# Two heads' softmax rows transposed side by side, and one reading engine per half of a PSUM bank

## The chip, the cores and the metric

The kernel runs on one core of one Trainium2 chip. The metric is the device time of one execution in microseconds (us), from the start of the program on the core to its end. The engines are named as the profile names them: PE (TensorE, the matrix engine; its weight loads are listed apart as PEld), DVE (VectorE), ACT (ScalarE), POOL (GpSimd) and SP (SyncE, which issues transfers).

## What is computed

One decoder layer on 1024 tokens of width 1024, in float32: a normalisation with a shift and scale from a conditioning vector, one input projection, an attention group of 8 query heads that share 2 key/value heads (4 heads to each), a short gated convolution group, an output projection, and a feed-forward block. The attention has three branches, and the part that matters here is the product of each branch's probabilities with its values:

```
p_c = masked_softmax(q . kc * scale + bias_c)      # 63 compressed keys
p_s = masked_softmax(q . ks * scale + bias_s)      # the causal keys (with 16 blocks, all are selected)
p_w = masked_softmax(q . kw * scale + bias_w)      # the last 512 keys
o   = g0 * (p_c @ vc) + g1 * (p_s @ vs) + g2 * (p_w @ vw)
```

The gates g come from a sigmoid of the projection.

## The kernel before

Every product is made of float32r halves: a tensor is split into a rounded part (`hi`) and its remainder (`lo`), and the products of the parts are added in PSUM. V is kept with both parts side by side, 64 columns of `hi` and 64 of `lo`, so a product with V gives 128 rows, which are folded to 64 at the end.

All instructions are recorded by a planner (class `Plan`): each operation has a cost, the engines that may do it and the operations that it must follow. The planner makes a list schedule, and the instructions are then issued in that order on every engine. So a changed cost or a changed dependence moves instructions on all engines. A dependence is found in `op` (line 116) from the memory that the operations touch; for PSUM the whole bank counts as one place (line 77), and only a write makes a dependence (line 131). The cost of a matmul is set in `mm` (line 307), that of a transpose on PE in `pet` (line 314).

The attention works on units of one pair of heads `hp` (both heads of a pair share the same K and V) and 256 queries `m`. `attention` (line 1112) makes four rows for it: 128 queries each, two query blocks `qp` and two heads `hl`. `row` (line 924) makes the scores of one row on PE, adds the bias and finds the maximum on DVE, takes exp on ACT, scales by gate over sum on POOL or ACT, and returns the blocks: one of 64 keys (the compressed branch, on 64 partitions once transposed) and up to 13 of 128 keys, each with its block of V. The rows lie in a buffer that holds four of the longest. `pv` (line 983) then takes groups of up to four blocks: it transposes them on PE into one of two PSUM banks (`tp_r`: the banks `sc2` and `stb`), copies the bank as `hi` on ACT, subtracts for `lo` on DVE, and multiplies: for every block a product of V with 128 columns of `hi` and one with 128 of `lo`, all added into the bank `po`. At the end of a unit `po` is folded into the output with two copies on ACT and two additions on DVE. There are 16 such units (`supers`, line 1110).

While the rows go through DVE and ACT, PE is given other products in between: conv products with the first eight units, and the first half's output projection and 30 tiles of the first feed-forward product with the other eight (`products`, line 999). They accumulate into the banks `fa0`, `fa1` and `sc3`. The planner decides where each stands.

Ahead of the attention, `raws` (line 706) copies the raw K and V of the compressed branch from four PSUM banks: four copies from each bank, each copy on ACT or DVE as the planner chooses.

Of the kernel before, what the change touches and what calls it, by code (L numbers as in the profile page):

```python
# [14 lines left out]
PSUM = bass.MemoryType.PSUM  # L15
# [18 lines left out]
def f32(ap):  # L34
    return ap.bitcast(F)
# [11 lines left out]
class Plan:  # L47
# [68 lines left out]
    def op(self, alts, outs, ins, nbytes=0, port=(), weight=1):  # L116
        o = Op(alts, len(self.ops), nbytes)
        o.weight = weight
        o.port = port
        o.group = self.group  # L120
        for aps, wr in ((ins, False), (outs, True)):
            for ap in aps:
                if not hasattr(ap, "tensor"):
                    continue
                key = ap.tensor.name
                if ap.space == DRAM and key not in self.scratch:
                    continue
                m = self._mask(ap)
                log = self.mem.setdefault(key, [])
                for po, pm, pw in log:  # L130
                    if (wr or pw) and po is not o and self._hit(m, pm):
                        if po.end is None:
                            o.preds.add(po)
                        else:
                            o.past.append((po, *po.end))
                if wr:
                    log[:] = [e for e in log if e[0] is o or not self._covers(m, e[1])]
                log.append((o, m, wr))
        self.ops.append(o)
        return o  # L140
# [165 lines left out]

    def mm(self, out, a, b, start, stop):
        n, m = self._n(out), self._n(a)
        c = max(0.4375 * n + 3, 58.0)
        if a.dtype == F and n > 128:  # L310
            c *= 4
        self.op([("PE", c, lambda: self.nc.tensor.matmul(out, a, b, start=start, stop=stop))], [out], [a, b])  # L312
# [30 lines left out]
    def tt(self, out, a, b, op, engs=("DVE",)):  # L343
        n, alts = self._n(out), []
        for e in engs:
            if e == "DVE":
                alts.append((e, 1.04 * n + 68, lambda: self.nc.vector.tensor_tensor(out, a, b, op)))  # L347
            else:
                alts.append((e, 2.11 * n + 148, lambda: self.nc.gpsimd.tensor_tensor(out, a, b, op)))
        self.op(alts, [out], [a, b], port=("POOL",) if self._ps(a, b) else ("DVE", "POOL"))  # L350
# [91 lines left out]
def hymba_layer(ctx: ExitStack, tc: tile.TileContext, xT, cT, w_first, w_cols, w_vg, w_ada, w_ada2, b_ada,  # L442
# [3 lines left out]
    P = Plan(tc)  # L446
    P.ahead = AHEAD
    mult, add, subt, amax, amin = ALU.mult, ALU.add, ALU.subtract, ALU.max, ALU.min
# [59 lines left out]
    ident, qpair = FA2[:, FA2N - 640:FA2N - 512], RA[:, RAN - 128:]  # L508
# [3 lines left out]
    h = [[Region(RA, H0 + 8192 * hf + 4096 * i, H0 + 8192 * hf + 4096 * i + 4096)(8, 512) for i in range(2)] for hf in range(2)]  # L512
# [105 lines left out]
    acc = [[sc_t[0], sc_t[1]], [sc_t[2], sc_t[3]], fa_t]  # L618
# [23 lines left out]
    craws = [Cr(2, T) for _ in range(2)]  # L642
# [63 lines left out]
    def raws(i):  # L706

        for hf in range(2):
            for g in range(2):
                r, c = slice(64 * g, 64 * g + 64), 512 * hf  # L710
                P.copy(craws[i][0:64, g, c:c + 512], acc[i][hf][r], ("ACT", "DVE"))
                f = 1 - hf
                P.copy(craws[i][64:128, g, c - 1 + f:c + 511], acc[i][hf][r, f:512], ("ACT", "DVE"))

    def compress(i):
        craw, cpe = craws[i], cpe_r()
# [136 lines left out]
    while c0 < TROW:  # L853
        n = min(512, TROW - c0)
# [39 lines left out]
    def prow(w):  # L894
        if pb[0] + w > PB:
            pb[0] = 0
        pb[0] += w
        return pbuf[:, pb[0] - w:pb[0]]
# [25 lines left out]
    def row(hp, m, qp, hl, q):  # L924
        qt = 2 * m + qp
        tt, te, tg = tabs[2 * hp + hl]
        kall, kw0, _, vt, sc_r = half1 if m >= 2 else half0
        nf, w0 = 128 * (qt + 1), max(0, qt - 4)
        nw = 128 * (qt - w0 + 1)
        s = prow(64 + nf + nw)  # L930
        mx, nm, den, cf = mx_r(), nm_r(), den_r(), cf_r()

        tab0, te0 = 896 - 128 * qt, 64 + nf
        cmp = (64, tg[:, 56 - 8 * qt:120 - 8 * qt], 0, 0)

        def full(a, b):
            return b - a, tt(tab0 + a, tab0 + b), 64 + a, 1

        if qt in (3, 7):
            jobs = [([(KC0 + a, 512)], [full(a, a + 512)]) for a in range(0, nf, 512)]  # L940
            last = [(0, 64)], [cmp]
        else:
            n0 = min(nf, 448)
            jobs = [([(0, 64 + n0)], [cmp, full(0, n0)])]
            last = ([(512, nf - n0)], [full(n0, nf)]) if nf > n0 else ([], [])
        if qt >= 4:
            jobs.append(([(kw0 + 128 * w0 + 128, 512)], [(512, tt(512, 1024), te0 + 128, 2)]))
            te_ = [(kw0 + 128 * w0, 128)], [(128, te, te0, 2)]
            if sum(n for _, n in last[0]) <= 384:
                last = last[0] + te_[0], last[1] + te_[1]  # L950
            else:
                jobs.append(te_)
        else:
            jobs.append(([(kw0, nw)], [(nw, tt(tab0, tab0 + nw), te0, 2)]))
        seen = set()
        for mms, sums in jobs + [last]:
            if not mms:
                continue
            a, c = sc_r(), 0
            for k0, n in mms:  # L960
                for i in range(2):
                    P.mm(a[:, c:c + n], q[:, hl, i, qp * 128:qp * 128 + 128], kall[:, k0:k0 + n], i == 0, i == 1)
                c += n
            c = 0
            for n, tab, ro, br in sums:
                P.ttr(s[:, ro:ro + n], a[:, c:c + n], tab, mx[:, br:br + 1] if br in seen else 2 * NEG, mx[:, br:br + 1])
                seen.add(br)
                c += n
        P.ts(nm, mx, -1.0, -0.1 * NEG, mult, amin, engs=EW)
        rs = [slice(0, 64), slice(64, 64 + nf), slice(64 + nf, 64 + nf + nw)]  # L970
        for br in (1, 2, 0):
            P.act(s[:, rs[br]], s[:, rs[br]], AF.Exp, bias=nm[:, br:br + 1], accum=den[:, br:br + 1])
        P.ts(den, den, 1e-30, 0.0, amax, add, engs=EW)
        P.recip(cf, den)
        P.tt(cf, cf, gates[:, qt, (2 * hp + hl) * 3:(2 * hp + hl) * 3 + 3], mult, EW)
        for br in (1, 2, 0):
            P.ts(s[:, rs[br]], s[:, rs[br]], cf[:, br:br + 1], 0.0, mult, add, engs=("POOL", "ACT"))
        vF, vW = ([vt[:, k, b] for k in range(qt + 1)] for b in range(2))
        return [(s[:, rs[1]][:, 128 * k:128 * k + 128], vF[k]) for k in range(qt + 1)] + \
            [(s[:, rs[0]], vc[hp // 2][0:64])] + \  # L980
            [(s[:, rs[2]][:, 128 * (k - w0):128 * (k - w0) + 128], vW[k]) for k in range(w0, qt + 1)]

    def pv(oo, blocks):

        parts = [b for b in blocks if b[0].shape[-1] == 128]
        parts = [[b for b in blocks if b[0].shape[-1] < 128]] + [parts[i:i + 4] for i in range(0, len(parts), 4)]
        for gi, part in enumerate(parts):
            n, w = 128 * len(part), part[0][0].shape[-1]
            tp, hi, lo = tp_r()[0:w, 0:n], hl_r()[0:w, 0:n], hl_r()[0:w, 0:n]
            for i, (p, _) in enumerate(part):  # L990
                P.pet(tp[:, 128 * i:128 * i + 128], p, ident)
            P.copy(hi, tp)
            P.sub(lo, tp, f32(hi))
            for i, (_, v) in enumerate(part):
                c = slice(128 * i, 128 * i + 128)
                P.mm(oo, v, hi[:, c], gi + i == 0, False)
                P.mm(oo, v, lo[:, c], False, gi == len(parts) - 1 and i == len(part) - 1)

# [113 lines left out]
    def attention(hp, m, q):  # L1112

        acc = po_r()
        o = at0[hp][:, 256 * m:256 * m + 256] if m < 2 else ot_r()
        for i in range(4):
            pv(acc[:, 128 * i:128 * i + 128], row(hp, m, i % 2, i // 2, q))
        for hl in range(2):
            r, c = slice(64 * hl, 64 * hl + 64), slice(256 * hl, 256 * hl + 256)
            P.copy(o[r], acc[r, c])  # L1120
            P.tt(o[r], acc[64 - 64 * hl:128 - 64 * hl, c], o[r], add)
        if m >= 2:
            c = 256 * (m - 2)
            hi, lo = (h[1][i][:, 4 + hp, c:c + 256] for i in range(2))
            P.copy(hi, o, ("ACT", "DVE"))
            P.sub(lo, o, f32(hi), EW)
# [5 lines left out]
    for u, (hp, ms) in enumerate(supers):  # L1132
# [9 lines left out]
        for m in ms:  # L1142
            q = q_r()
# [45 lines left out]
    with ExitStack() as pf:  # L1189
# [32 lines left out]
        for ch in range(4):  # L1222
            for j in range(8):
                w = load_w(w_ff1[ch * 8 + j])
# [10 lines left out]
            for c in range(8):  # L1235
                w = load_w(w_ff2[ch, c])
# [90 lines left out]
```

## Time and profile before

| | us |
|---|---|
| median of 3 runs (1434.29 to 1435.71) | 1435.21 |
| the profiled execution's own time | 1435.77 |
| its span, first to last instruction | 1434.0 |
| PE busy (share of the span) | 1397.4 (97%) |
| DVE busy | 781.6 (55%) |
| ACT busy | 644.8 (45%) |
| mean granted TensorE clock | 0.987 |

The span falls into stages: to about 75 us the normalisation and the first products; to 215 us the compression, the window keys, values and queries; from 215 to 830 us the attention with the other products in between; to 885 us the rest of the second half's output projection; and then the feed-forward block to the end. A matmul's row in the trace gives its start and how long it is in the array; since several are in the array at a time, the price of one is read from the distance between starts, and not from that duration.

### The profile page before, as it was taken

The page shows a single profiled execution, that of the slowest core. Times are in us where ns is not written, and L with a number is a line of the kernel's source. Part 1 is how long each engine was busy: PE and PEld are TensorE (multiplying, and loading weights), DVE is VectorE, ACT ScalarE, POOL GpSimd, SP SyncE. Part 2 cuts the span into 40 slices and gives each one's busy share as a digit, 9 for nine tenths or more (in the row PEclk, how much of TensorE's full clock was granted, in tenths as well). Part 3 has the DMA queues.
Part 4 walks back from the last instruction along what each step waited for, and adds up shares of the span by engine and source line. Part 5 has one row for each costly group of instructions (what it writes and reads, how often), then busy time and mean ns, then how long its engine had stood idle before and what let it go on. Part 6 is the DMA issues. An engine that isn't in the chain of part 4 may idle for free.

```text
span 1434.0 us, 19643 instructions
## 1 busy us (share of the span) xinstructions
PE 1397.4 (97%) x7016; PEld 1141.2 (80%) x7016; DVE 781.6 (55%) x1928; ACT 644.8 (45%) x1362; POOL 114.3 (8%) x221
## 2 busy tenths in 40 slices
PE   5999999999999999999999997999999999999998
PEld 2778777887887888888888886888888888888887
DVE  5987876667576686555555457451531352243122
ACT  5776656665465676655755545330130122103110
POOL 0001001111121111101111100000000000000000
PEclk8999999999999999999999998999999999999999
DMA  9478884353252213433322541450430232123031
GB/s 346 129 216 239 288 265 155 103 163 106 69 185 75 90 40 96 148 121 98 110 84 82 176 133 67 146 169 30 127 109 30 75 119 72 59 69 106 32 118 59
DMA packets 91606, 175.72 MB, mean 123 GB/s; under 512 B 10745, under 2 KB 30754, under 8 KB 90996
## 3 DMA queue, kind: packets, MB, share of 16 engines
q1 hardware_dynamic: 87764, 159.65, 34.3%
q0 software_dynamic: 3744, 14.81, 3.3%
q8 instruction: 55, 0.90, 0.3%
q14 instruction: 43, 0.35, 0.1%
HBM read 145.48 MB, written 32.61 MB: 124 GB/s over the span
## 4 chain that ended last, share of the span: by engine, by line
PE 90%; DMA 4%; DVE 2%; ACT 1%; issue 1%; SPq 1%; DVEq 0%; ACTq 0%
PE pd L312 37%; PE fa L312 23%; PE sc L312 16%; PE po L312 9%; PE stb L315 3%; PE sc L315 2%; DMA d_tab<-d_row 1%; ACT FA L330 1%; DVE FA L358 1%; DVE RA L347 1%; DMA FA<-in_w_cols 1%; SPq L397 1%; DMA FA<-in_w_ada 1%; DVE FA L347 0%; DMA FA<-in_xT 0%
## 5 line engine op out<-in xcount | busy, mean ns | idle before, releaser
L312 PE MATMUL fa<-RA 128*128 128x512 f32 (+1 forms) x1384 | 463.3, 419 | 1.1 <-DVE RA L347 1.1
L312 PE MATMUL pd<-RA 128*128 128x512 f32 x1392 | 413.8, 393 | 7.4 <-ACT RA L336 4.3
L336 ACT CAST RA<-FA 128x512 fp32r<-128x512 f32 (+5 forms) x235 | 163.0, 708 | 491.8 <-PE pd L312 286.3
L312 PE MATMUL sc<-RA 128*128 128x512 f32 (+6 forms) x1328 | 357.3, 371 | 12.0 <-DVE RA L338 9.8
L347 DVE TENSOR_TENSOR RA<-FA,RA 128x512 fp32r<-128x512 f32 (+5 forms) x327 | 246.7, 773 | 166.6 <-PE pd L312 95.5
L312 PEld LDWEIGHTS pd<-RA 128*128 128x128 f32 x1392 | 262.4, 190 | 66.3 <-ACT RA L336 5.0
L312 PE MATMUL pd<-hid,RA 128*128 128x512 f32 x960 | 310.4, 389 | 0.0
L312 PEld LDWEIGHTS fa<-RA 128*128 128x128 f32 (+1 forms) x1384 | 250.6, 190 | 42.6 <-DVE RA L347 1.6
L312 PEld LDWEIGHTS sc<-RA 128*128 128x128 f32 x1328 | 236.1, 191 | 54.2 <-DVE RA L338 10.6
L312 PEld LDWEIGHTS pd<-hid,RA 128*128 128x128 f32 x960 | 180.2, 188 | 37.4
L312 PE MATMUL po<-RA 128*128 128x128 f32 (+1 forms) x1092 | 206.4, 266 | 0.1
L312 PEld LDWEIGHTS po<-RA 128*128 128x128 f32 (+1 forms) x1092 | 185.4, 193 | 18.0 <-DVE RA L347 0.5
L358 DVE SCALAR_TENSOR_TENSOR FA<-pd,mod,FA 128x512 f32<-128x512 f32 x64 | 46.4, 748 | 199.5 <-PE pd L312 199.5
L330 ACT ACTIVATE FA<-FA,nm 128x64 f32<-128x64 f32 (+6 forms) x192 | 114.6, 599 | 31.5 <-DVE nm L366 31.5
L377 DVE CUSTOM_DVE_ANT_0 FA<-sc,FA 128x512 f32<-128x512 f32 (+5 forms) x192 | 82.8, 455 | 43.3 <-PE sc L312 41.9
L330 ACT ACTIVATE FA<-FA 128x512 f32<-128x512 f32 (+2 forms) x147 | 89.1, 618 | 21.3 <-DVE FA L358 11.7
L347 DVE TENSOR_TENSOR RA<-stb,RA 128x512 fp32r<-128x512 f32 (+4 forms) x108 | 60.7, 562 | 47.3 <-PE po L312 29.4
L315 PE MATMUL stb<-FA,FA 128*128 128x128 f32 (+1 forms) x332 | 84.3, 283 | 0.0
L370 POOL TENSOR_SCALAR FA<-FA,cf 128x64 f32<-128x64 f32 (+8 forms) x97 | 59.5, 620 | 200.1 <-DVE cf L347 150.3
L336 ACT CAST RA<-sc 64x128 fp32r<-64x128 f32 (+3 forms) x108 | 44.4, 411 | 68.2 <-PE sc L315 54.8
L336 ACT CAST RA<-stb 128x512 fp32r<-128x512 f32 (+4 forms) x108 | 52.1, 483 | 48.0 <-PE po L312 30.3
L347 DVE TENSOR_TENSOR RA<-sc,RA 64x128 fp32r<-64x128 f32 (+3 forms) x108 | 50.8, 470 | 33.5 <-ACT RA L336 28.0
(123 smaller groups left out, 961.5 us busy)
## 6 DMA issues: line engine op xcount, KB each, us to landing
FA<-in_w_ff SPq DMA_DIRECT2D x64, 512.0 KB, 4.3
FA<-in_w_ada SPq DMA_DIRECT2D x64, 256.0 KB, 3.1
FA<-in_w_ff SPq DMA_DIRECT2D x60, 256.0 KB, 2.7
FA<-in_w_cols SPq DMA_DIRECT2D x34, 256.0 KB, 3.4
FA<-in_xT SPq DMA_DIRECT2D x32, 256.0 KB, 5.0
FA<-in_w_ada SPq DMA_DIRECT2D x16, 512.0 KB, 5.6
d_q<-FA SPq DMA_DIRECT2D x32, 256.0 KB, 4.7
RA<-d_q POOLq DMA_DIRECT2D x16, 512.0 KB, 4.7
```

Source lines behind the costliest of these rows:

```text
L312: self.op([("PE", c, lambda: self.nc.tensor.matmul(out, a, b, start=start, stop=stop))], [out], [a, b])
L315: self.op([("PE", 110.0, lambda: self.nc.tensor.transpose(out, a, ident))], [out], [a, ident])
L330: self.op([("ACT", c, lambda: self.nc.scalar.activation(out, a, func, **kw))], outs, ins)
L336: alts.append((e, 0.833 * n + (53 if ps else 93), lambda: self.nc.scalar.copy(out, a)))
L347: alts.append((e, 1.04 * n + 68, lambda: self.nc.vector.tensor_tensor(out, a, b, op)))
L358: self.op([("DVE", 1.04 * self._n(out) + 68 + 61 * ptr, lambda: self.nc.vector.scalar_tensor_tensor(out, a, s, b, op0, op1, **kw))], [out] ...
L370: alts.append((e, 0.833 * n + 174 + 83 * ptr, lambda: self.nc.gpsimd.tensor_scalar(out, a, s1, s2, op0, op1)))
L377: self.op([("DVE", 1.04 * self._n(out) + 75, lambda: self.nc.vector.tensor_tensor_reduce(out, a, b, 1.0, init, ALU.add, ALU.max, accum))], ...
L397: self.op([(q, c, lambda: e.dma_start(out=out, in_=a))], [out], [a], nbytes=n, weight=2 if within else 1)
```

## The change

`pv` now takes the rows of both heads of one query block. A group is two blocks of each head (four transposes into one bank), with the two heads' transposed blocks side by side, and each product streams 256 columns, 128 of either head, against the block of V that both share. `attention` calls it twice for a unit instead of four times, and the fold reads strided halves of `po`. In `raws` the copies from one half of a bank's partitions are all on ACT, those from the other all on DVE. The planner counts two readers of one PSUM bank as dependent, in the order in which they are recorded, and takes 110 instead of 58 as the least cost of a matmul.

```
@@ Plan.op @@
-                    if (wr or pw) and po is not o and self._hit(m, pm):
+                    if (wr or pw or ap.space == PSUM) and po is not o and self._hit(m, pm):
@@ Plan.mm @@
-        c = max(0.4375 * n + 3, 58.0)
+        c = max(0.4375 * n + 3, 110.0)
@@ raws @@
-                P.copy(craws[i][0:64, g, c:c + 512], acc[i][hf][r], ("ACT", "DVE"))
+                e = (("ACT",), ("DVE",))[g]
+                P.copy(craws[i][0:64, g, c:c + 512], acc[i][hf][r], e)
                 f = 1 - hf
-                P.copy(craws[i][64:128, g, c - 1 + f:c + 511], acc[i][hf][r, f:512], ("ACT", "DVE"))
+                P.copy(craws[i][64:128, g, c - 1 + f:c + 511], acc[i][hf][r, f:512], e)
@@ pv @@
-    def pv(oo, blocks):
-
-        parts = [b for b in blocks if b[0].shape[-1] == 128]
-        parts = [[b for b in blocks if b[0].shape[-1] < 128]] + [parts[i:i + 4] for i in range(0, len(parts), 4)]
+    def pv(oo, rows):
+
+        wide = [i for i, (p, _) in enumerate(rows[0]) if p.shape[-1] == 128]
+        parts = [[i for i, (p, _) in enumerate(rows[0]) if p.shape[-1] < 128]]
+        parts += [wide[i:i + 2] for i in range(0, len(wide), 2)]
         for gi, part in enumerate(parts):
-            n, w = 128 * len(part), part[0][0].shape[-1]
+            n, w = 256 * len(part), rows[0][part[0]][0].shape[-1]
             tp, hi, lo = tp_r()[0:w, 0:n], hl_r()[0:w, 0:n], hl_r()[0:w, 0:n]
-            for i, (p, _) in enumerate(part):
-                P.pet(tp[:, 128 * i:128 * i + 128], p, ident)
+            for i, k in enumerate(part):
+                for hl in range(2):
+                    c = 256 * i + 128 * hl
+                    P.pet(tp[:, c:c + 128], rows[hl][k][0], ident)
             P.copy(hi, tp)
             P.sub(lo, tp, f32(hi))
-            for i, (_, v) in enumerate(part):
-                c = slice(128 * i, 128 * i + 128)
+            for i, k in enumerate(part):
+                v, c = rows[0][k][1], slice(256 * i, 256 * i + 256)
                 P.mm(oo, v, hi[:, c], gi + i == 0, False)
                 P.mm(oo, v, lo[:, c], False, gi == len(parts) - 1 and i == len(part) - 1)
@@ attention @@
-        for i in range(4):
-            pv(acc[:, 128 * i:128 * i + 128], row(hp, m, i % 2, i // 2, q))
+        for qp in range(2):
+            pv(acc[:, 256 * qp:256 * qp + 256], [row(hp, m, qp, hl, q) for hl in range(2)])
+        a4, o3 = acc.rearrange("p (q h i) -> p q h i", q=2, h=2), o.rearrange("p (q i) -> p q i", q=2)
         for hl in range(2):
-            r, c = slice(64 * hl, 64 * hl + 64), slice(256 * hl, 256 * hl + 256)
-            P.copy(o[r], acc[r, c])
-            P.tt(o[r], acc[64 - 64 * hl:128 - 64 * hl, c], o[r], add)
+            r = slice(64 * hl, 64 * hl + 64)
+            P.copy(o3[r], a4[0:64, :, hl])
+            P.tt(o3[r], a4[64:128, :, hl], o3[r], add)
```

The whole program has 1184 products into `po` from transposed rows before (1056 over 128 keys, 128 over the 64 keys of the compressed branch) and 592 now (528 and 64). The transposes are 592 in both.

On PE, in the first attention unit, before. `po` is the sum of a unit, `vc` the compressed branch's V (its products contract over 64 partitions), `fa_188` a bank of the products in between, `stb` a bank of transposes, `sc_183` one of scores; a row's shape is that of its output:

```order
L312 MATMUL fa_188<-RA 128x512 x2
L312 MATMUL po<-RA,vc_137 128x128
L312 MATMUL fa_188<-RA 128x512
L312 MATMUL po<-RA,vc_137 128x128
L315 MATMUL stb<-FA_179,FA_175 128x128
L312 MATMUL sc_183<-RA 128x512
L312 MATMUL po<-RA 128x128 x2
L315 MATMUL stb<-FA_179,FA_175 128x128
```

The same engine in the first unit, now:

```order
L312 MATMUL po<-RA 128x256 x2
L312 MATMUL fa_188<-RA 128x512
L312 MATMUL po<-RA 128x256
L312 MATMUL po<-RA,vc_137 128x256
L312 MATMUL fa_188<-RA 128x512
L312 MATMUL po<-RA,vc_137 128x256
L315 MATMUL stb<-FA_179,FA_175 64x128
```

The products with `po` are half as many and twice as wide; other products still stand between them. Over the whole order the 128 products with `vc` stand in 109 separate runs before, and the 64 now in 57.

On DVE and ACT where `raws` reads the banks `sc_183` and `sc_184`, before, DVE first:

```order
L347 TENSOR_TENSOR RA<-FA_175,RA 128x512
L338 COPY FA_179<-sc_183 64x512
L338 COPY FA_179<-sc_184 64x512
L338 COPY FA_179<-sc_183 64x511
L338 COPY FA_179<-sc_184 64x512
L347 TENSOR_TENSOR RA<-FA_179,RA 128x2x256
```

ACT in the same place, before:

```order
L336 CAST RA<-FA_179 128x2x256 x2
L336 COPY FA_179<-sc_183 64x512
L336 COPY FA_179<-sc_184 64x512 x2
L336 COPY FA_179<-sc_183 64x511
L336 COPY FA_175<-fa_187 128x512
```

ACT there now:

```order
L336 CAST RA<-FA_179 128x2x64 x2
L336 COPY FA_179<-sc_184 64x512
L336 COPY FA_179<-sc_183 64x512
L336 COPY FA_179<-sc_184 64x512
L336 COPY FA_179<-sc_183 64x511
L336 CAST RA<-FA_179 128x2x256 x2
```

And DVE there now:

```order
L347 TENSOR_TENSOR RA<-FA_179,RA 128x2x64
L367 TENSOR_SCALAR qns<-qnr 128x1
L338 COPY FA_179<-sc_184 64x512
L338 COPY FA_179<-sc_183 64x512
L338 COPY FA_179<-sc_184 64x512
L338 COPY FA_179<-sc_183 64x511
L347 TENSOR_TENSOR RA<-FA_179,RA 128x2x256
```

Before, either engine read both banks while the other did; now ACT alternates between the two banks for its four copies, and in the plan DVE's two of a bank follow ACT's two of it.

## Rows read from the trace of the kernel before

**Rows 1.** The page: busy time, share of the span, number of instructions.

```profile
PE 1397.4 (97%) x7016; PEld 1141.2 (80%) x7016; DVE 781.6 (55%) x1928; ACT 644.8 (45%) x1362; POOL 114.3 (8%) x221
```

**Rows 2.** Windows: length, busy us (instructions) per engine, granted clock, DMA share, GB/s.

```profile
core 0: us, PE busy (x) PEld busy (x) DVE busy (x) ACT busy (x) POOL busy (x), PEclk, DMA share, GB/s
75.00:215.00 140.00, 133.12 (x679) 111.33 (x679) 109.80 (x261) 91.05 (x203) 11.78 (x23) 0.98 0.85 256
215.00:425.00 210.00, 210.00 (x1177) 169.90 (x1176) 139.15 (x475) 125.51 (x362) 40.32 (x87) 0.99 0.39 127
425.00:550.00 125.00, 123.48 (x729) 103.53 (x729) 92.13 (x273) 80.81 (x178) 19.96 (x32) 1.00 0.24 78
550.00:830.00 280.00, 280.00 (x1658) 233.54 (x1657) 155.38 (x459) 163.36 (x354) 40.59 (x66) 1.00 0.36 118
```

**Rows 3.** Windows of 25 us: two with much DVE work, one of the feed-forward block.

```profile
500.00:525.00 25.00, 24.88 (x165) 20.96 (x163) 21.73 (x68) 18.78 (x40) 3.36 (x7) 1.00 0.19 61
525.00:550.00 25.00, 24.82 (x151) 21.22 (x151) 20.82 (x66) 19.93 (x46) 5.75 (x8) 1.00 0.13 43
...
975.00:1000.00 25.00, 25.00 (x112) 20.67 (x112) 5.00 (x6) 2.10 (x2) 0.00 (x0) 1.00 0.13 42
```

**Rows 4.** Waits of PE from 215 to 830 us.

```profile
engine line waited for: us in total, times, longest us
PE fa L312 <- DVE RA L347: 1.1, 1, 1.1
PE po L312 <- DVE FA L347: 0.2, 1, 0.2
```

**Rows 5.** Groups of PE from 215 to 830 us, by form: rows*columns of weights, moving shape.

```profile
L312 PE MATMUL po<-RA 128*128 128x128 f32 x1056 | 198.4, 264 | 0.1
...
L312 PE MATMUL po<-RA,vc 64*128 64x128 f32 x128 | 37.4, 316 | 0.2 <-DVE FA L347 0.2
```

**Rows 6.** Timeline of PE: start us, length us, what, count of the run.

```profile
604.98 0.34 PE L312 MATMUL po<-RA 128*128 128x128 f32 x2
...
605.52 0.22 PE L312 MATMUL po<-RA 128*128 128x128 f32 x1
605.58 0.45 PE L312 MATMUL fa<-RA 128*128 128x512 f32 x1
605.86 0.22 PE L312 MATMUL po<-RA 128*128 128x128 f32 x1
```

**Rows 7.** Timeline of PE around two products with the compressed branch's V.

```profile
611.06 0.32 PE L312 MATMUL po<-RA,vc 64*128 64x128 f32 x1
611.32 0.50 PE L312 MATMUL fa<-RA 128*128 128x512 f32 x1
611.75 0.32 PE L312 MATMUL po<-RA,vc 64*128 64x128 f32 x1
```

**Rows 8.** Timeline of PE, a 256-column product of scores.

```profile
375.64 0.28 PE L312 MATMUL sc<-RA 128*128 128x256 f32 x1
```

**Rows 9.** Timeline of PE, 375.85 us on: the run of the matmul after it.

```profile
375.76 0.54 PE L312 MATMUL sc<-RA 128*128 128x512 f32 x2
```

**Rows 10.** Timelines of ACT and DVE in the raw copies; brackets: idle before, releaser.

```profile
68.81 1.07 ACT L336 COPY FA<-sc 64x512 f32<-64x512 f32 x2 [0.86 <-DVE FA L338]
...
67.50 1.28 DVE L338 COPY FA<-sc 64x512 f32<-64x512 f32 x2 [0.38 <-ACT FA L336]
...
69.91 1.28 DVE L338 COPY FA<-sc 64x511 f32<-64x511 f32 x2 [1.13 <-ACT FA L336]
```

**Rows 11.** Instructions on tiles po and stb: min/median/max ns, first and last start, forms.

```profile
L336 ACT COPY FA<-po x35: 262/367/563, 71.1 to 830.4; 64x256 f32<-64x256 f32 x32, 8x512 f32<-8x512 f32 x1, 126x256 f32<-126x256 f32 x1, 64x126 f32<-64x126 f32 x1
L347 DVE TENSOR_TENSOR FA<-po,FA x34: 281/420/428, 101.9 to 831.3; 64x256 f32<-64x256 f32 x32, 126x256 f32<-126x256 f32 x1, 64x126 f32<-64x126 f32 x1
...
L336 ACT CAST RA<-stb x108: 244/568/593, 213.6 to 827.6; 128x512 fp32r<-128x512 f32 x64, 128x256 fp32r<-128x256 f32 x16, 64x128 fp32r<-64x128 f32 x16, 128x384 fp32r<-128x384 f32 x8
```

## The prediction

> **What bounds the kernel now.** The first view is the page's list of busy times: PE is busy for 97% of the span, DVE for 55%, ACT for 45% [rows 1]. That alone proves little, since the lengths of matmuls overlap, so the second view is the windows by stage. From 215 to 830 us PE shows no gap but 1.5 us between 425 and 550 us, at a granted clock of 0.99 to 1.00 (the 2.4 GHz level), while DVE is busy 139.2 + 92.1 + 155.4 = 386.7 of the 615 us (63%) and ACT 369.7 (60%) [rows 2]. The tightest stretch for the others is 500 to 550 us, where DVE has 42.6 of 50 us and ACT 38.7 [rows 3]. Third come the waits: in all these 615 us PE waited for another engine for 1.3 us [rows 4]. So in the attention stage the end is set by what PE is given to do, and a matmul taken out is time taken out as long as the others keep up. In the feed-forward block PE does 112 products of 512 columns in 25 us [rows 3], and the change does nothing there.
>
> **What one product costs.** The lengths in the groups (264 ns for a 128-column product) are latencies. The price is the distance between starts. A product of 512 columns costs 25/112 = 0.223 us [rows 3]. From one `po` to the next with one such product between them it is 605.86 - 605.52 = 0.34 us, which leaves 0.117 for the `po`; a run of two `po` is 0.34 long against 0.22 for one, so the second adds 0.12 [rows 6]. I take 0.115, as both are rounded. For 256 columns there is one clean pair: a product of scores starts at 375.64 and the next matmul at 375.76 [rows 8, 9], so 0.12. Twice the columns cost nearly the same: 512 columns in 0.223 us make 0.056 for 128 columns, so the 128-column product is held to 0.115 by something other than its columns, most likely by its weight load.
>
> The products with the compressed branch's V are another kind. They contract over 64 partitions, and with one product of 512 columns between them two of them are 611.75 - 611.06 = 0.69 us apart [rows 7]. That leaves 0.69 - 0.223 = 0.47 for the narrow one, four times the 0.115 of a full one. I read it as a price of going over to another height of weights and back, paid by each run of narrow products and not by each product.
>
> **The change part by part.**
>
> *Products over 128 keys.* Before 1056 [rows 5] x 0.115 = 121.4 us, now 528 x 0.12 = 63.4. Gain 58.0.
>
> *Products over the 64 compressed keys.* 128 [rows 5] in 109 runs before: 109 x 0.47 + 19 x 0.115 = 53.4 us. Now 64 in 57 runs, each run dearer by the 128 further columns, which nothing hides at a change of height: 57 x (0.47 + 0.056) + 7 x 0.12 = 30.8. Gain 22.6. The trace of before has no narrow product of 256 columns; the bounds are a gain of 26.6 if the columns are hidden (57 x 0.47) and of 7.0 if the price of going over stays at its old total (128 x 0.115 - 64 x 0.12).
>
> *Transposes.* 592 before and now, the same shapes: nothing.
>
> *Copies and subtractions of the transposed banks.* The columns are the same, the instructions 48 fewer on ACT and on DVE (216 to 168 each), since a group now takes four transposes of one width more often. At 0.24 us for the smallest copy, of 128 columns, and 0.57 for 512 [rows 11], an instruction less with the same columns is about 0.13 us: 6 us on each engine, none of it on the path, as PE sets the end.
>
> *Folding `po`.* Two copies (0.37 us) and two additions (0.42) [rows 11] for each of 16 units; now they stand one after the other in the plan, 1.58 us against 1.2 if one copy ran beside an addition. `po` is one bank, so the next unit's products queue behind it; PE has other products to do meanwhile. 0, at worst 16 x 0.4 = 6 us.
>
> *Raw copies.* Before, ACT and DVE are made to wait for each other there, 0.86, 0.38 and 1.13 us, while both read the same banks [rows 10]: readers of one bank evidently take turns whatever the plan thinks. The new plan knows that, and gives the halves out so that each engine works through its own. It can give back up to 2.4 us; but DVE takes eight copies in place of six (0.64 each by the same rows, 1.3 us), in a stage where it is busy 78% of the time [rows 2]. I take 0, between -2.4 and +1.3.
>
> *Pairing of rows.* A pair's transposes wait for both rows, where one row was enough. What hides it is the work in between: the order of the new program still has other products between the `po` products. I take 0 for the wait itself; the case in which the cover is gone is a rival below.
>
> *What comes back.* With 80.6 us less on PE (58.0 + 22.6) the 615 us become about 534, and the old slack of the other engines shrinks: DVE goes to some 380 of 534 us, 71%. In the stretch of 500 to 550 us PE's part would shrink by 13% to 43.5 us while DVE alone has 42.6 [rows 3]; nothing packs that closely, so I give 3 us back there. For the rest there are two rows to go between: the attention stage, where PE waits 1.3 us with DVE at 63% [rows 4], and 75 to 215 us, where PE lacks 6.9 of 140 us (4.9%) with DVE at 78% and the DMA queues at 0.85 [rows 2]. Half way between in DVE's load would be 2.5 to 3%, but the DMA share here stays below 0.4, so I take 1.7% of 534 = 9 us. Together 12, between 0 and 29 (3 + 4.9% of 534).
>
> There was more hidden slack than the trace shows: the old plan counted 58 ns for a product that takes 115 (and 470 for the narrow ones), so PE ran late against its plan and everything was ready when it came. The new plan's 110 is nearly right. That speaks for some waits, and is the second reason for the 12.
>
> **Sum.** 1435.8 (the profiled execution's own time; the median of the three runs is 0.6 lower) - 58.0 - 22.6 + 12 = 1367.2. I forecast **1367 us**.
>
> **Rivals.**
>
> 1. *PE runs dry now and then.* With the plan exact and DVE at 71%, PE waits as it does from 75 to 215 us: 29 us come back, 1384; if the narrow products also gain only 7.0, 1400. For it: the 500 to 550 us stretch. Against it: half of PE's order in this stage is other products, free of the rows. 0.18 for 1378 to 1400.
> 2. *Nothing comes back*, and the narrow products gain their 26.6, with 2.4 from the raw copies: 1435.8 - 58.0 - 26.6 - 2.4 = 1349. For it: 1.3 us of waits in 615. 0.15 for 1346 to 1356.
> 3. *The columns are the price, so that a wide product costs as two.* Then one product of 256 columns would take 2 x 0.115 = 0.23, only changes of height would be saved, and the time is 1435.8 - 22.6 = 1413 or more, up to no change at all. Against it stands the 0.12 of rows 8 and 9; for it, only that this is one pair in another accumulation. 0.03, of which 0.02 within 0.2% of before. The Trainium skill has the rule for the far end of this, in "TensorE: Matmul & The Clock Gate", section "Back-to-back issue gap": a warm matmul takes N/2.4 + 2.5 ns, which is 56 ns for 128 columns and 109 for 256. By that rule 1184 products of the one kind and 592 of the other differ by an estimated 1.5 us, and the time would not change. The trace disagrees: 115 and not 56 ns.
> 4. *Slower: the pairs starve PE.* If at each of the 32 pairs PE had to sit until the second row is ready, and nothing lay between, it would lose up to a row's share of the stage, 615/64 = 9.6 us. The point at which this turns the gain into a loss is 80.6/32 = 2.5 us for each pair; at half a row (4.8 us) it is 154 us, and the time 1435.8 - 80.6 + 154 = 1509. Against it: the rows buffer holds four rows, so the next pair is made while one is multiplied, and other products stand between. 0.03.
>
> **How the numbers follow.** The forecast's own range, 1356 to 1378, has 0.58. Rivals 1 to 4 have 0.18, 0.15, 0.03 and 0.03; 0.03 is left for something between 1400 and 1432. The range of 8 in 10 is 1348 to 1396: it leaves out the slow end of rival 1, the fast end of rival 2 and rivals 3 and 4. A measurement of this kernel can tell about 0.2% (3 us) from no change. Faster by more than that 0.95, within it 0.02, slower 0.03.
>
> **What would show it.** The stage from the first transpose to the feed-forward block is 65 to 72 us shorter and the feed-forward block is as long as before. In the timeline a `po` of 256 columns and a product of 512 between two of them make about 0.34 us, as with 128 columns now; if they make 0.45, rival 3 is right. A narrow one with a product of 512 makes about 0.75 us; if it is near 0.69 the columns are hidden, and if it is near 1 us the narrow gain is gone. The waits of PE in the stage sum to some 12 us by DVE or ACT; over 25, rival 1 is right. What would make the forecast wrong altogether is a long gap of PE in the attention stage with `stb` or `sc` transposes behind it: then the rows, and not PE, set the pace.

## The result and the profile after

The changed kernel takes 1371.14 us (median of 4 runs, 1366.74 to 1372.64) against 1435.43 in the same measurement; the ratio is 0.9549, with a 95% interval of 0.9524 to 0.9573. That is 64.3 us less, where the sum had 68.6 (58.0 + 22.6 - 12). The profiled execution took 1369.85 us, with a span of 1368.1. The page after, the line of busy times that answers to [rows 1]:

```profile
span 1368.1 us, 18289 instructions
...
PE 1326.0 (97%) x6424; PEld 1080.7 (79%) x6424; DVE 777.8 (57%) x1882; ACT 623.2 (46%) x1293; POOL 134.9 (10%) x240
```

PE is as dense as before, with 592 matmuls fewer (7016 to 6424), and its busy time is down by 71.4 us. DVE and ACT have nearly the same work in a shorter span. The windows by stage of the kernel after, as in [rows 2]; the attention stage lies between 205 and 765 us, the feed-forward block from 820 (a line `...` marks lines left out):

```profile
core 0: us, PE busy (x) PEld busy (x) DVE busy (x) ACT busy (x) POOL busy (x), PEclk, DMA share, GB/s
75.00:205.00 130.00, 125.64 (x633) 104.06 (x632) 105.98 (x238) 81.74 (x181) 12.30 (x23) 0.97 0.87 260
205.00:415.00 210.00, 209.54 (x1125) 170.04 (x1124) 158.10 (x520) 133.40 (x365) 54.11 (x99) 1.00 0.46 149
415.00:515.00 100.00, 97.95 (x526) 80.96 (x525) 77.12 (x220) 69.66 (x148) 18.79 (x29) 0.98 0.27 84
515.00:765.00 250.00, 250.00 (x1389) 207.53 (x1388) 154.82 (x451) 157.96 (x339) 48.02 (x75) 1.00 0.40 128
...
820.00:1368.00 548.00, 538.51 (x2367) 442.96 (x2367) 198.57 (x284) 113.29 (x149) 0.00 (x0) 0.99 0.29 89
```

DVE is busy for 158.1 + 77.1 + 154.8 = 390 of the 560 us of the attention stage (70%, from 63%), and PE still shows no gap in the second half of it. The feed-forward block is as long as before: its first matmul starts at 884.55 us before and at 818.93 now, 65.6 us earlier, which is nearly the whole difference of the spans (65.9):

```profile
884.55 0.79 PE L312 MATMUL pd<-RA 128*128 128x512 f32 x1 [2.85 <-DVE RA L338]
...
818.93 0.50 PE L312 MATMUL pd<-RA 128*128 128x512 f32 x1 [4.11 <-DVE RA L338]
```

One sign of the prediction did not come: the stretch from the first transpose to this point was to be 65 to 72 us shorter, and it is 96 us shorter (671.4 to 575.3). The first transpose of a row stands at 213.18 us before and at 243.68 now:

```profile
213.18 0.38 PE L315 MATMUL stb<-FA,FA 128*128 128x128 f32 x2
...
243.68 0.27 PE L315 MATMUL sc<-FA,FA 128*64 128x128 f32 x1
```

With the pairing alone (e1 below) it stands at 241.9, with the planner's parts alone (e2) at 209.7, so the pairing moves it. PE does other products in the meantime and is busy for all of the 40 us from 205 to 245, so the later start costs nothing by itself.

The waits of PE from 205 to 765 us, which answer to [rows 4]:

```profile
engine line waited for: us in total, times, longest us
PE sc L312 <- DVE mx L377: 1.7, 1, 1.7
PE fa L312 <- DVE RA L347: 0.5, 1, 0.5
PE stb L315 <- DVE RA L347: 0.3, 1, 0.3
```

2.5 us in place of 1.3: next to nothing of the 12 us that the prediction took off.

The prices of the new products can be read as in [rows 6] and [rows 7]. The timeline of PE after: two wide `po` with a product of 512 columns between them, and two narrow ones with two such products between them:

```profile
280.32 0.28 PE L312 MATMUL po<-RA 128*128 128x256 f32 x1
280.43 0.40 PE L312 MATMUL fa<-RA 128*128 128x512 f32 x1
280.66 0.28 PE L312 MATMUL po<-RA 128*128 128x256 f32 x1
...
694.41 0.38 PE L312 MATMUL po<-RA,vc 64*128 64x256 f32 x1
694.72 0.73 PE L312 MATMUL fa<-RA 128*128 128x512 f32 x2
695.38 0.38 PE L312 MATMUL po<-RA,vc 64*128 64x256 f32 x1
```

The wide cycle is 280.66 - 280.32 = 0.34 us, as foreseen: twice the columns in the same time. The narrow one is 0.97 - 2 x 0.223 = 0.52 us, where the sum had 0.526.

In the raw copies the waits of [rows 10] did not go away, they were gathered. DVE in the kernel after:

```profile
68.60 2.61 DVE L338 COPY FA<-sc 64x512 f32<-64x512 f32 x4 [2.40 <-ACT FA L336]
```

Three waits of 0.86, 0.38 and 1.13 us (2.4 in all, on both engines) have become one of 2.40 on DVE.

### The profile page after: what moved, and what is told of

Read it like the earlier page. It is cut to its first block, busy times and chain, and to the rows that moved or that the text cites. A ratio compares the mean times of both kernels' runs of the same rounds, so it can differ in the third digit from the quotient of the medians.

```text
span 1368.1 us, 18289 instructions
## 1 busy us (share of the span) xinstructions
PE 1326.0 (97%) x6424; PEld 1080.7 (79%) x6424; DVE 777.8 (57%) x1882; ACT 623.2 (46%) x1293; POOL 134.9 (10%) x240
## 4 chain that ended last, share of the span: by engine, by line
PE 90%; DMA 4%; DVE 4%; ACT 1%; SPq 1%; issue 0%; DVEq 0%; ACTq 0%
PE pd L312 38%; PE fa L312 24%; PE sc L312 16%; PE po L312 7%; PE stb L315 3%; PE sc L315 2%; DVE FA L358 1%; DMA FA<-in_w_ada 1%; DVE FA L347 1%; DMA d_k<-FA 1%; ACT FA L330 1%; SPq L397 1%; DMA FA<-in_cw 1%; DMA d_tab<-d_row 1%; DVE RA L347 1%
## 5 line engine op out<-in xcount | busy, mean ns | idle before, releaser
L336 ACT CAST RA<-FA 128x512 fp32r<-128x512 f32 (+6 forms) x235 | 162.3, 706 | 487.2 <-PE pd L312 292.5
L312 PE MATMUL sc<-RA 128*128 128x512 f32 (+7 forms) x1328 | 354.9, 370 | 14.3 <-DVE RA L338 12.1
L312 PE MATMUL po<-RA 128*128 128x256 f32 (+2 forms) x564 | 139.8, 303 | 1.4 <-DVE RA L347 1.4
L330 ACT ACTIVATE FA<-FA,nm 128x64 f32<-128x64 f32 (+5 forms) x192 | 114.7, 600 | 18.1 <-DVE nm L366 17.7
L312 PEld LDWEIGHTS po<-RA 128*128 128x128 f32 (+1 forms) x564 | 101.8, 191 | 12.9 <-ACT RA L336 1.7
L377 DVE CUSTOM_DVE_ANT_0 FA<-sc,FA 128x64 f32<-128x64 f32 (+5 forms) x192 | 84.8, 455 | 40.6 <-PE sc L312 39.2
L347 DVE TENSOR_TENSOR RA<-stb,RA 128x512 fp32r<-128x512 f32 (+1 forms) x84 | 53.3, 635 | 36.4 <-PE po L312 17.8
L315 PE MATMUL sc<-FA,FA 128*128 128x128 f32 (+1 forms) x288 | 69.8, 277 | 0.0
L347 DVE TENSOR_TENSOR RA<-sc,RA 128x512 fp32r<-128x512 f32 (+2 forms) x84 | 51.0, 607 | 25.9 <-ACT RA L336 21.4
L336 ACT CAST RA<-stb 128x512 fp32r<-128x512 f32 (+1 forms) x84 | 45.2, 538 | 40.6 <-PE stb L315 39.7
```

The lines of the kernel that those rows point to most:

```text
L315: self.op([("PE", 110.0, lambda: self.nc.tensor.transpose(out, a, ident))], [out], [a, ident])
L330: self.op([("ACT", c, lambda: self.nc.scalar.activation(out, a, func, **kw))], outs, ins)
L336: alts.append((e, 0.833 * n + (53 if ps else 93), lambda: self.nc.scalar.copy(out, a)))
L377: self.op([("DVE", 1.04 * self._n(out) + 75, lambda: self.nc.vector.tensor_tensor_reduce(out, a, b, 1.0, init, ALU.add, ALU.max, accum))], ...
```

## Experiments

The forecast was near, but the profile already said that one of its terms, the 12 us of waits, was not there; so another had to be too large. The theory on record was: 58.0 us from the wide products, 22.6 from the narrow ones, 12 us back in waits, because the other engines' slack is used up. The rival formed from the trace after: nothing comes back, and the products of 128 columns had been priced too high, since a transpose behind one of them makes it cheaper.

**Either half of the change alone.** First the pairing without the planner's parts, then the planner's parts and raw copies without the pairing:

```
 e1:  if (wr or pw) and po is not o and self._hit(m, pm):        # as before
      c = max(0.4375 * n + 3, 58.0)                              # as before
      P.copy(craws..., ("ACT", "DVE"))                           # as before
 e2:  pv and attention as before, the other hunks of the diff kept
```

> The pairing of the two heads alone: the planner's dependence between readers of a bank, its least cost of a matmul and the raw copies are as before. If the whole gain is PE's own price of fewer and wider products, 1371 (1367 to 1376), as with the full change. If the planner's parts bring the 2.4 us of the raw copies or more, 1374 to 1385. If the nearly exact plan is what costs waits (the 12 us that the prediction took off), it is faster than the full change: 1359 to 1366.

Measured: 1370.01 us, ratio 0.9548 (0.9531 to 0.9565). The pairing alone is the whole gain.

> The planner's parts and the raw copies alone, the products with V as before (1184 of 128 columns). If they only move instructions and PE sets the end, 1435 (1431 to 1438). If the old order was bad because it counted 58 ns for a product that takes 115, some 1420 to 1430. If a nearly exact plan costs waits, 1438 to 1447.

Measured: 1433.07 us, ratio 0.9986 (0.997 to 1.0002). The planner's parts are worth 2 us, between 4 us and nothing, which cannot be told from zero, and the nearly exact plan does not cost time.

**The height of the weights.** The narrow products are made 128 rows high, before and after:

```
-            [(s[:, rs[0]], vc[hp // 2][0:64])] + \
+            [(s[:, 0:128], vc[hp // 2])] + \
```

(`pv` then finds that block by its V and not by its width.) The 64 further columns of the row are the first probabilities of the next branch; they meet rows of `vc` that are zero.

> The kernel before, with the compressed branch's 64 keys padded to 128 by the next 64 columns of the row, against rows of V that are zero: the same sums, but no product contracts over 64 partitions. If going over to another height of weights and back is what makes a narrow product cost 0.47 us for each run, 109 x 0.47 + 19 x 0.115 = 53.4 us become 128 x 0.115 = 14.7: 1435.4 - 38.7 = 1397 (1392 to 1402). If its price has another cause (the bank po, the wait ahead of it), 1432 to 1436.

Measured: 1403.22 us, ratio 0.978 (0.9762 to 0.9798), so 31.6 us less than before (29 to 34), a little less than the 38.7 expected.

> The same padding in the changed kernel. By the price of going over, 57 x 0.526 + 7 x 0.12 = 30.8 us become 64 x 0.12 = 7.7: 1371.1 - 23.1 = 1348 (1343 to 1353). If PE is by now held up by DVE and ACT in the attention stage, only part of it comes: 1355 to 1366. If the price has another cause, 1368 to 1373. Against the kernel before with the same padding, the wide products and the slots saved give 58.0 + 7.0 = 65 us by the prediction's prices without waits, 53 with its 12 us of waits, and 51 if a product of 128 columns next to a transpose costs less than 0.115 (44 + 7).

Measured: 1350.79 us, ratio 0.9409 (0.9392 to 0.9425), 20.1 us under the changed kernel by the two ratios (0.0140 x 1435.4), with some 4 us either way. The timeline of PE in this kernel, two of the padded products with a transpose and a product of 512 columns between them:

```profile
529.85 0.28 PE L312 MATMUL po<-RA,vc 128*128 128x256 f32 x1
529.97 0.27 PE L315 MATMUL sc<-FA,FA 128*128 128x128 f32 x1
530.00 0.48 PE L312 MATMUL fa<-RA 128*128 128x512 f32 x1
530.32 0.28 PE L312 MATMUL po<-RA,vc 128*128 128x256 f32 x1
```

The cycle is 0.47 us. Less 0.223 for the product and 0.11 for the transpose, the product with `vc` now costs 0.14, in place of 0.52. So the height was the cause of its price. (The padding also widens the transposes of this block from 64 columns of weights to 128. That is not where the price was: in the trace before, a transpose of either width behind a product of 512 columns ends 109 ns after it.) The price is 31.6 / 109 = 0.29 us for a run before and 20.1 / 57 = 0.35 after, on top of a full product's; the sum had 0.355 (0.47 - 0.115) and 0.41. By these runs the change itself, by taking 109 runs to 57, got 31.6 - 20.1 = 11.5 us from this, with some 5 us either way.

**By the run or by the product.** The two narrow products of a group are issued one right behind the other, so the 64 of them stand in 32 runs, not 57:

```
+                if gi == 0:
+                    P.both(oo, v, hi[:, c], lo[:, c])     # one recorded operation, two matmuls
+                    continue
```

> The changed kernel, with the two products of the compressed branch in each group issued one right behind the other: 64 of them as before, but in 32 runs in place of 57. If the price of going over to 64 partitions and back is paid by each run, as the prediction put it, 25 runs fewer at the 20.4 / 57 = 0.36 us that the padding in the changed kernel showed: 1371 - 9 = 1362 (1358 to 1366). If each product pays it, 1371 (1368 to 1375).

Measured: 1363.29 us, ratio 0.9488 (0.946 to 0.9516); 0.0061 x 1435 = 8.8 us less than the change, with some 5 us either way, where 9 were expected by the run and none by the product. It is paid by the run. The trace of the kernel before says the same: in the 19 places where one narrow product follows another, its end comes 111 ns after the other's, against 113 for two full ones.

**The width alone.** Order and pairing as in the changed kernel, but each wide product over 128 keys is issued as two halves:

```
+                    P.halves(oo, v, hi[:, c], False)      # one recorded operation, two matmuls of 128 columns
+                    P.halves(oo, v, lo[:, c], ...)
```

> The changed kernel, in the same order and with the same pairing, but each of the 528 products over 128 keys is issued as two of 128 columns, one right behind the other. This undoes the width alone. At the prediction's flat prices (0.115 for each half, 0.12 for the whole) it costs 528 x 0.11 = 58 us: 1429 (1425 to 1433). If a 128-column product is cheaper where a transpose follows it (205 of the 528 places), as the distances between ends in the trace say (0.074 us more there and 0.107 elsewhere), it costs 15.2 + 34.6 = 50 us: 1421 (1417 to 1425). If the pairing and not the width brought the gain, 1371 to 1380.

Measured: 1424.97 us, ratio 0.9927 (0.9898 to 0.9955), 0.0378 x 1435.4 = 54 us more than the change, with some 5 us either way. The width is what brought most of the gain. The other 10 us are no more than what the fewer narrow products and runs account for, so nothing is left over for the pairing as such. But 54 lies between 50 and 58, and the time does not tell the two prices apart. The traces speak for the lower one, below.

**The slack of the other engines.** DVE is given the subtraction for `lo` twice, in 76 of the 168 groups and in all of them:

```
             P.sub(lo, tp, f32(hi))
+            if gi % 2:                       # e6; without this line e7
+                P.sub(lo, tp, f32(hi))
```

> The changed kernel, with the subtraction for lo made twice in 76 of the 168 groups: DVE has some 52 us more in the attention stage, 79% in place of 70%, and the planner knows. If waits come with DVE's load as the prediction took it from the stage at 75 to 215 us (4.9% at 78%), 20 to 27 us: 1390 to 1398. If PE stays fed as long as DVE has room, 1371 (1367 to 1376).

Measured: 1374.09 us, ratio 0.9566 (0.9547 to 0.9585).

> The same in all 168 groups: some 107 us more on DVE, 89% of the attention stage. By the prediction's relation of waits to load, over 50 us: 1420 or more. If PE stays fed as long as DVE has room, 1371 to 1380. In between if DVE is short only in the tight stretch around 475 to 500 us.

Measured: 1376.89 us, ratio 0.9592 (0.957 to 0.9614). By the page DVE is busy for 859.2 us in e7, 81 more than in the changed kernel (some 107 were expected); they cost 0.0043 x 1435 = 6 us, with some 5 us either way. The windows of that last kernel, attention stage:

```profile
core 0: us, PE busy (x) PEld busy (x) DVE busy (x) ACT busy (x) POOL busy (x), PEclk, DMA share, GB/s
205.00:415.00 210.00, 209.64 (x1146) 172.50 (x1144) 184.17 (x597) 141.02 (x386) 46.98 (x99) 1.00 0.47 151
415.00:515.00 100.00, 94.45 (x537) 77.22 (x535) 94.58 (x261) 62.58 (x134) 19.49 (x32) 0.99 0.24 73
515.00:765.00 250.00, 249.92 (x1327) 206.11 (x1326) 186.49 (x489) 152.28 (x318) 55.36 (x76) 0.99 0.40 128
```

DVE is busy 465 of 560 us (83%) and PE lacks 6.0 us in all, 5.6 of them in the stretch where DVE is at 94.6 of 100 (2.5 and 2.1 in the changed kernel). Outside of it DVE goes from 68% to 81%, and PE lacks 0.4 us in 460, as it does in the changed kernel.

**Copies merged in the padded kernel.** With equal heights the compressed block can go into the groups of two:

```
-        parts = [[i for i, (_, v) in enumerate(rows[0]) if v is vc[0] or v is vc[1]]]
-        parts += [wide[i:i + 2] for i in range(0, len(wide), 2)]
+        wide = list(range(len(rows[0])))
+        parts = [wide[i:i + 2] for i in range(0, len(wide), 2)]
```

> The padded kernel, with the compressed block taken into the groups of two like the others: 8 groups fewer, and no group that is half as wide, so some 30 copies and subtractions are merged on ACT and DVE. PE's work is the same. If PE sets the end throughout, as with the padding alone: 1351 (1347 to 1354). If ACT and DVE hold it up in places, 1340 to 1347.

Measured: 1350.35 us, ratio 0.9408 (0.938 to 0.9436): the same as with the padding alone, which is what was expected if PE sets the end. The changed kernel with the padding (e4, e9) beats both the kernel before and the changed one.

## Why the prediction was right, point by point

**What bounds the kernel** was right: PE does, before and after. Taking PE's work away takes time away (e1, e4, e8), giving it back brings it back (e5), and keeping DVE busy for 81 us more hardly matters (e7).

**The wide products were priced too high before.** The step that failed is "I take 0.115" for each of the 1056: it was read between a `po` and a product behind it, and taken for all. The timeline of the kernel before has another kind of place:

```profile
613.10 0.22 PE L312 MATMUL po<-RA 128*128 128x128 f32 x1
613.16 0.28 PE L315 MATMUL sc<-FA,FA 128*128 128x128 f32 x1
613.19 0.48 PE L312 MATMUL fa<-RA 128*128 128x512 f32 x1
613.50 0.34 PE L312 MATMUL po<-RA 128*128 128x128 f32 x2
```

From `po` to `po` there are 0.40 us; without the 0.223 of the product and the 0.11 of the transpose, 0.07 are left for the `po`, and not 0.115. Over the whole trace, from 200 us on, the median distance between the ends of two successive matmuls is (ends as the profile models them; in brackets how often; narrow is a product with `vc`):

```
 ns, from end to end             before          after
 512 columns, then po             60 (365)       119 (270)
 po, then 512 columns            284 (371)       233 (169)
 po, then po                     113 (393)       119 (117)
 po, then a transpose            130 (233)       109 (205)
 512 columns, then a transpose   109 (184)       109 (195)
 transpose, then po               61 (225)       121 (97)
 512 columns, then narrow        254 (63)        312 (40)
 narrow, then narrow             111 (19)        119 (7)
 narrow, then 512 columns        428 (59)        426 (18)
 narrow, then a transpose        259 (28)        260 (30)
```

A `po` of 128 columns takes 60 ns itself and adds 54 to a product behind it (284 against 230 between two products of 512 columns in this stage). To a transpose behind it it adds 21 at the median, 16 in the mean (125 against 109). The successor's weights seem to count: behind a `po`, a transpose with 64 columns of weights ends after 109 ns (16 places), as it does behind a product of 512 columns, and one with 128 after 131 (217 places). That fits with the prediction's guess at the weight load, but no run varies the load by itself.

So a `po` of 128 columns costs 0.114 where a product follows and 0.076 where a transpose does, in 233 of the 1056 places: 1056 x 0.114 - 233 x 0.038 = 111.5 us, where the sum had 121.4. With 528 x 0.12 = 63.4 now, the gain is 48 us and not 58.

The trace of e5 agrees with this rather than with the flat price. Take every distance up to the feed-forward block at the median of its pair of kinds in its own trace, and call the sum PE's need: it is 813 us in e5 and 763 in the changed kernel, so 50 us more (50 by the prices above, 58 by the flat one). The other 4 of its 54 us are distances above their medians. This price is read from traces; no run settles it by its time.

**The narrow products** were the right mechanism and the right gain. By the table a run costs 194 ns more than a full product where it begins (254 against 60; 193 now) and 129 to 144 where it ends (259 against 130, 428 against 284; 151 to 193 now). Summed over all places that is 36 us before (0.33 for a run) and 21 now (0.36), so both prices of the sum (0.355 and 0.41) were somewhat too dear, and their difference is 15 us where the sum had 22.6 - 7.0 = 15.6. The 20.1 us of e4 agree with the 21; the 31.6 of e3 are short of the 36, and e3's trace has the need 36 us lower and 3 us more above the medians. By the times of e3 and e4 alone the fall from 109 to 57 brought 11.5 us, give or take 5, and the wide products and the saved narrow ones together 64.7 - 11.5 = 53 us (65 by the sum: 58.0 + 7.0; 55 with 48). A small slip stands in the bound of 26.6: with the 7 narrow products inside runs it is 25.8.

**What comes back** was wrong in the attention stage: 12 us were taken off, 9 of them by DVE's load, and there PE waits 2.5 us in place of 1.3. Summed as above, PE's need up to the feed-forward block falls from 834 to 763 us, about the 48 + 15 + 7 us of the prices. What goes beyond the medians is 46 us before and 51 after: 10.4 and 9.1 of them in the attention stage (from 200 us on, to 830 and 765), and the 5 more stand almost wholly ahead of it, where the prediction looked for none. The step that failed is the interpolation by DVE's load between two stages. Of the 6.9 us that PE lacks from 75 to 215 us, 6.6 lie in three single waits (3.0, 2.0 and 1.6 us), which is no share that grows with DVE's load. With DVE at 83% the whole kernel was 6 us slower here (e7), and not the 5% of the stage (26 us) that the interpolation's upper end had; and e2 shows that the argument from the old plan's wrong prices was empty as well.

So two errors of opposite sign stand behind a forecast that is 4 us off: some 10 us too much gain in the wide products, and some 7 of the 12 us that did not come back (none in the stage where they were looked for). That they nearly cancel is luck; the mechanism of either gain was right without it.

**Raw copies and planner**: taken at 0, and not told from 0 by e2, though not as described: the two engines still wait for each other for 2.4 us. The longest wait of PE ahead of the attention is 9.8 to 10.3 us in the three kernels without the new dependence (before, e1, e3) and 12.1 to 12.7 in three with it (after, e2, e4). The cause of this stays open.

**The rivals.** That nothing comes back (rival 2) was right for the attention stage, but its sum, 1349, was not, since it kept the price of the wide products above and took the upper bound for the narrow ones. Rival 1 (waits) fell with e6 and e7. Rival 3 (columns are the price) fell with the 0.34 us cycle and e5. Rival 4 (starved by the pairs) did not show: no wait of PE from 205 to 765 us is longer than 1.7 us, and the 30 us by which the first transposes come later are filled with other products.

## What to carry to other kernels

On an engine that is full, price an operation by the distance between starts with and without it, at each kind of neighbour, and not only in the cleanest place of the trace: here the price of a product depended on what stood behind it. Look for instructions whose price is far off their kind's; a product that differs in height cost four times its share, and padding it with zeros (e4) brought as much again as a third of the change. Waits that a tighter schedule "should" bring need a mechanism with a place; a share taken over from another stage is none.

## What the runs showed of the hardware

Going over from weights of 128 rows to 64 and back costs 0.29 to 0.36 us for each run, whatever the number of products in it (e3, e4, e8), at a granted clock of 0.99 to 1.00 in their attention stages. This agrees with the Trainium skill, "TensorEngine Tiling (Array Packing)", section "Key Properties", which says that a change of tiling mode drains the engine; it gives no time for it, and the traces here show the time and not the draining. A product of 256 columns costs 0.12 us and one of 128 the same 0.11 to 0.12 ahead of another product, but 0.08 ahead of a float32 transpose of 128 columns, and the 0.06 that it takes itself ahead of one of 64. And ACT and DVE waited for each other where both only read the same PSUM banks, for 2.4 us in one place, whether the planner knew of it or not; whether the banks or the program's own semaphores ask for that, no run shows.
